# The mixer's output projection: its first two blocks as one pair, with three units of seven products, and the chunk ring's spare tiles kept on the raw side until the last block

## The chip, the cores and the metric

The kernel runs on one core of a Trainium2 chip. The metric is the device time of the whole program in microseconds (us). Engines are named as in the profile: PE is the matrix engine (PEld its weight loads), DVE the vector engine, ACT the scalar engine, POOL the GpSimd engine, SP the engine that only issues transfers.

## The reference

One layer of a decoder trunk on 256 tokens of width 2048, in float32. Cut to what the change touches:

```python
merged = sigmoid(gA) * (o_a @ w_o_mla) + sigmoid(gB) * (o_b @ w_o_swa)   # 256 x 2048
y = merged @ w_out                                                       # 2048 x 2048 weights
x = x + rms_norm(y, norm_mix_post)
x = x + rms_norm(conv_ffn(rms_norm(x, norm_ffn_pre), w_up, conv_w, conv_b, w_down), norm_ffn_post)
```

Everything before it (input projection, two attentions, gates) and after it (a gated feed-forward block of width 5632) stays as it is.

## The kernel before

**Products in three passes.** Each float32 operand is held as a high part and a low part. `mm3` (lines 173 to 177) makes one product from three matmuls: high x high (L175), high x low (L176), low x high (L177). A weight chunk of 128 x 1024 goes through four hands: a DMA issued by SP brings it into a tile `raw` (L131); ACT copies it to `whi` (L143); DVE subtracts to get `wlo` (L144); PE uses both.

**The ring.** `raw`, `whi` and `wlo` come in turn from one pool: three `raw` tiles (RAW), four of each of the others (RING), and two more tiles of a tag `flex`. While `flex[0]` is "raw" these two serve as a fourth and fifth `raw` tile; when it is "w", they serve as one more `whi` and one more `wlo` turn. In the kernel before, `flex` is "raw" up to the output projection and is set to "w" ahead of its first block.

**gemm** multiplies all 256 tokens (two tiles of 128, `acc[0]` and `acc[1]`) with 512 columns: 8 chunks of two 128-row slices, 96 matmuls of 512 columns, and a `tick()` after each chunk. `at(t, f)` hands a piece of work over to a later tick, so transposes and evacuations are written between the chunks.

**pair_gemm** exists already, for the gates and for the down projection. It computes 1024 columns at once, with four accumulators `c` (tokens x column halves) and four more, `q`, in the other PSUM banks. Its `order` string lists units of 256 weight rows: "p" is a plain unit (2 rows of chunks x 4 products of three matmuls, 24 matmuls), "s" a unit of seven products (21 matmuls, a Strassen-like scheme). A unit of seven needs sums of the activations made ahead (`token_sums`), loads its two chunks `even` and `odd` by POOL's queue (L227, L228), and has DVE make four sums of weight halves (L232 to L235). At the end of the last unit of seven, `first_sums` and `more_sums` add the `q` accumulators up (L255 to L261).

**The stages around the change.** In the merge stage each of four blocks `j` multiplies the attention output with `w_o_mla` (gemm), while `merge_loads` fetches the gate `lta` and the other branch `lyb` by POOL's queue (L943, L944); DVE combines them with the accumulator (L955, L956); `m_cols` transposes the result on PE (L935, tile `mT`) and splits it into `mth`, `mtl` (tiles `ahl`). Then come four blocks of 512 columns of `w_out`, each a gemm; `y_evac` squares the accumulator on ACT and multiplies it on DVE with the gain `gpost` into `yg` (L972, L973). `gpost` (four transfers) and the residual `x2` (eight) are loaded by SP's queue during the first half of the merge stage (`late_loads`). In the last block all of token tile 0 is done first and token tile 1 after it, so its weights are held; its first three chunks use tiles of their own (pool `px`). `resid` then makes the residual, its transposes and the norm. The engine queues are in order; the tile framework lists each engine's rows by its own priorities, so a row can stand earlier than its place in the text.

Of the kernel before, what the change touches and what calls it, by code (L numbers as in the profile page):

```python
# [23 lines left out]
KT = D // P  # L24
# [17 lines left out]
def trunk_layer(ctx, tc, x, x_cols_in, conv_cols_in, g_mix_post, g_ffn_post, w_in, w_q, w_kv,  # L42
                sinks, rel, wo_a, wo_b, w_out, w_up, w_down, rope_tab, strip_sel, out):
    nc = tc.nc
    vec, act, pe, pool = nc.vector, nc.scalar, nc.tensor, nc.gpsimd

    def open_pool(name, bufs=1, **kw):
        es = ExitStack()
        return es, es.enter_context(tc.tile_pool(name=name, bufs=bufs, **kw))
# [3 lines left out]
    pss = ctx.enter_context(tc.tile_pool(name="pss", bufs=2, space=PS))  # L53
# [5 lines left out]
    def sb(pl, shape, name, dt=F32, tag=None, bufs=None):  # L59
        return pl.tile(shape, dt, name=name, tag=tag or name, **({"bufs": bufs} if bufs else {}))  # L60
# [43 lines left out]
    flex = ["raw"]  # L104
    turn = dict(raw=0, w=0)
# [49 lines left out]
    now = [0]  # L155

    def at(t, *fs):
        steps[max(t, now[0])].extend(fs)
# [6 lines left out]
    def drain():  # L165
        while steps:
            tick()
# [11 lines left out]
    def gemm(xh, xl, w, k0, nk, c0, n, split=None, extra=None, ps=None):  # L179

        kc = 1024 // n if n in (256, 512) else 2
        acc = new_acc("g", ps)
        todo = []
        cuts = list(range(0, nk, kc)) + [nk]
        for ci, (k, ke) in enumerate(zip(cuts[:-1], cuts[1:])):
            kk = ke - k
            src = w[(k0 + k) * P:(k0 + k + kk) * P, c0:c0 + n].rearrange("(a p) n -> p a n", p=P)
            hi, lo = wchunk(src, [kk, n], *(extra or {}).get(ci, ()))
            for j in range(kk):
                kt = k + j  # L190
# [473 lines left out]
    acc, _ = gemm(XH, XL, w_in, 0, KT, 0, 512)  # L664
# [4 lines left out]
    acc, _ = gemm(XH, XL, w_in, 0, KT, C_KV, KVR + ROPE)  # L669
# [78 lines left out]
    AH, AL = pair_view(ath), pair_view(atl)  # L748
# [138 lines left out]
    b = now[0] + 26  # L887
# [11 lines left out]
    for j in range(4):  # L899
        acc, _ = gemm(XH, XL, w_in, 0, KT, C_GA + 512 * j, 512)  # L900
# [16 lines left out]
    gpost = sb(p6, [P, D], "gpost", tag="gp")  # L917

    def late_loads(i):

        if i < 4:
            nc.sync.dma_start(gpost[:, i * 512:(i + 1) * 512], g_mix_post[i * 512:(i + 1) * 512].partition_broadcast(P))
        else:
            t, j = divmod(i - 4, 4)
            nc.sync.dma_start(x2[t][j], x[t * P:(t + 1) * P, j * 512:(j + 1) * 512])

    esx, px = open_pool("px", bufs=EXTRA)
    es4, p4 = open_pool("p4")

    def m_cols(p, ld):  # L930
        pt = pst.tile([P, 512], F32, name=f"mT{p}", tag="t")
        for i in range(2):
            for t in range(NT):
                c = (2 * (p % 2) + i) * P
                pe.transpose(pt[:, i * 256 + t * P:i * 256 + (t + 1) * P], ld[t][0][:, c:c + P], ident)  # L935
        split_to(mth[p][:, :], mtl[p][:, :], pt, 0.5)
# [8 lines left out]
            ld.append((a, b))  # L945
        return ld

    for i in range(12):
        at(now[0] + 10 + 2 * i, lambda i=i: late_loads(i))
    for j in range(4):  # L950
        ld = merge_loads(j)
        acc, _ = gemm(AH, AL, wo_a, 0, KT, 512 * j, 512)
        for t in range(NT):
            a, b = ld[t]
            vec.scalar_tensor_tensor(a, a, 1.0, acc[t], op0=ALU.add, op1=ALU.mult)  # L955
            vec.tensor_tensor(a, a, b, op=ALU.add)  # L956
# [4 lines left out]
    yg_all = [[sb(p6, [P, 1024], f"yg_{t}_{j}", tag="f" + "ab"[t], bufs=2) for j in range(2)] for t in range(NT)]  # L961
    yg = [[yg_all[t][j // 2][:, (j % 2) * 512:(j % 2 + 1) * 512] for j in range(4)] for t in range(NT)]
    blocks = [(0, 512), (512, 512), (1024, 512), (1536, 256), (1792, 256)]
    NB = len(blocks)
    W_BLOCKS = [(512 * j, 512) for j in range(4)]
    ssy = [sb(p3, [P, 4], f"ssy{t}") for t in range(NT)]
    jk = lambda name: sb(p6, [P, 512], name, tag="jk", bufs=1)

    def y_evac(acc, b, t):
        c0, n = W_BLOCKS[b]  # L970
        j, o = c0 // 512, c0 % 512
        act.activation(jk(f"yj{b}_{t}")[:, :n], acc[t][:, :n], AF.Square, accum_out=ssy[t][:, b:b + 1])  # L972
        vec.tensor_tensor(yg[t][j][:, o:o + n], acc[t][:, :n], gpost[:, c0:c0 + n], op=ALU.mult)  # L973

    x2hl = [slot("b", p) for p in range(8)]
    HH, HL = pair_view(highs(x2hl)), pair_view(lows(x2hl))
# [31 lines left out]
        vec.tensor_scalar(r2, r, 0.5, None, op0=ALU.mult)  # L1008
        rf[t] = (r, r2)

    flex[0] = "w"
    turn.update(raw=0, w=0)
    for b in range(4):
        c0, n = W_BLOCKS[b]
        last = b == 3
        acc, todo = gemm(MH_, ML_, w_out, 0, KT, c0, n, split=0 if last else None, extra={i: (px,) for i in range(EXTRA)} if last else None)
        if b == 0:
            drain()
            es4.close()
            es8, p8 = open_pool("p8")  # L1020
        if last:
# [311 lines left out]
EXTRA = 3  # L1333
# [69 lines left out]
```

## Time and profile before

| | |
|---|---|
| median of 3 runs | 1468.9 us (1468.19 to 1469.03) |
| the profiled execution: its own time | 1470.05 us |
| its span, first to last instruction | 1468.3 us |
| granted PE clock in it | 0.998 |
| PE busy in the span | 1456.9 us (99%), 7576 matmuls |
| DVE busy | 1067.2 us (73%) |
| ACT busy | 830.5 us (57%) |
| the 32 loads of `w_out`, first and last issue | 623.9 us and 709.2 us |

The profile gives the engines' busy time by group of instructions, what ended an engine's idle time, and the chain of work that ended last. A matmul's record is longer than its share of PE's time, because matmuls overlap, so PE's pace is read from the starts of matmuls that follow each other, not from the length of one.

### The profile page before, as it was taken

What the parts mean: (1) busy time and instruction counts of PE and PEld (TensorE: products, weight loads), DVE (VectorE), ACT (ScalarE), POOL (GpSimd) and SP (SyncE); (2) the same over time, 40 slices, a digit from 0 to 9 for tenths busy, and PEclk for the clock granted to TensorE, in tenths of its full rate; (3) what the DMA queues carried; (4) which work ended last, traced back from release to release, by engine and by line L of the source; (5) the groups of instructions that cost most, each with busy time, mean ns of one, the idle gap of its engine ahead of it and who ended that gap; (6) DMA issues with size and microseconds to landing.
All of it is one profiled execution on the core that took longest, in us unless ns stands there. A gap on an engine that the chain in (4) does not pass through costs nothing.

```text
span 1468.3 us, 20938 instructions
## 1 busy us (share of the span) xinstructions
PE 1456.9 (99%) x7576; PEld 1244.8 (85%) x7576; DVE 1067.2 (73%) x1881; ACT 830.5 (57%) x1372; POOL 64.9 (4%) x113
## 2 busy tenths in 40 slices
PE   9999999999999999999999999999999999999997
PEld 7888888888888888888888888888888888888886
DVE  7688896745667665555699976778776687677775
ACT  7588874543555554444566655555454565555453
POOL 0011110000000000000000000000000000000000
PEclk9999999999999999999999999999999999999999
DMA  8755376466655559756766666665656666667573
GB/s 297 211 164 167 108 259 192 162 212 200 191 156 160 164 163 334 226 184 212 225 205 185 188 193 193 187 187 187 218 174 213 198 187 189 187 197 233 163 237 129
DMA packets 149909, 287.60 MB, mean 196 GB/s; under 512 B 18428, under 2 KB 29597, under 8 KB 149677
## 3 DMA queue, kind: packets, MB, share of 16 engines
q1 hardware_dynamic: 141312, 256.80, 56.5%
q0 software_dynamic: 8400, 29.41, 6.4%
q8 instruction: 59, 0.97, 0.3%
q14 instruction: 46, 0.37, 0.1%
q10 hardware_dynamic: 92, 0.05, 0.0%
HBM read 277.79 MB, written 8.44 MB: 195 GB/s over the span
## 4 chain that ended last, share of the span: by engine, by line
PE 97%; DVE 2%; ACT 1%; issue 0%; DMA 0%; DVEq 0%; ACTq 0%
PE accg L175 13%; PE accg L177 13%; PE accg L176 13%; PE ub L1147 10%; PE ua L1147 10%; PE ua L1151 5%; PE ub L1151 5%; PE cd L177 2%; PE cd L175 2%; PE cd L176 2%; PE cdb L175 1%; PE cdb L177 1%; PE cdb L176 1%; PE mpo L875 1%; PE cg L176 1%; PE cg L177 1%
## 5 line engine op out<-in xcount | busy, mean ns | idle before, releaser
L144 DVE TENSOR_TENSOR wlo<-raw,whi 128x1024 fp32r<-128x1024 f32 (+2 forms) x476 | 576.3, 1214 | 282.5 <-ACT whi L143 275.2
L143 ACT CAST whi<-raw 128x1024 fp32r<-128x1024 f32 (+2 forms) x476 | 494.7, 1043 | 427.5 <-PE accg L177 172.3
L175 PE MATMUL accg<-whi,ahl 128*128 128x512 f32 (+1 forms) x480 | 187.9, 392 | 0.0
L177 PE MATMUL accg<-whi,ahl 128*128 128x512 f32 (+1 forms) x480 | 185.6, 387 | 0.0
L176 PE MATMUL accg<-wlo,ahl 128*128 128x512 f32 (+1 forms) x480 | 184.8, 385 | 0.0
L1147 PE MATMUL ua<-ahl,whi 128*128 128x512 f32 x640 | 154.6, 391 | 0.0
L1147 PE MATMUL ub<-ahl,whi 128*128 128x512 f32 x640 | 154.6, 391 | 0.0
L175 PE MATMUL accg<-whi,bhl 128*128 128x512 f32 x378 | 148.2, 392 | 0.0
L177 PE MATMUL accg<-whi,bhl 128*128 128x512 f32 x378 | 147.4, 390 | 0.0
L176 PE MATMUL accg<-wlo,bhl 128*128 128x512 f32 x378 | 147.3, 390 | 0.0
L1147 PEld LDWEIGHTS ub<-ahl,whi 128*128 128x128 f32 x640 | 117.5, 188 | 22.9 <-ACT cc L1045 0.2
L1147 PEld LDWEIGHTS ua<-ahl,whi 128*128 128x128 f32 x640 | 117.6, 188 | 22.7
L177 PEld LDWEIGHTS accg<-whi,ahl 128*128 128x128 f32 x480 | 90.1, 188 | 18.0
L176 PEld LDWEIGHTS accg<-wlo,ahl 128*128 128x128 f32 x480 | 90.3, 188 | 15.6
L175 PEld LDWEIGHTS accg<-whi,ahl 128*128 128x128 f32 x480 | 90.3, 188 | 15.5
L1151 PEld LDWEIGHTS ub<-ahl,wlo 128*128 128x128 f32 x640 | 82.2, 191 | 3.2
L1151 PEld LDWEIGHTS ua<-ahl,wlo 128*128 128x128 f32 x640 | 82.2, 191 | 3.1
L1151 PE MATMUL ua<-ahl,wlo 128*128 128x256 f32 x640 | 83.7, 283 | 0.0
L177 PEld LDWEIGHTS accg<-whi,bhl 128*128 128x128 f32 x378 | 71.0, 188 | 14.8
L176 PEld LDWEIGHTS accg<-wlo,bhl 128*128 128x128 f32 x378 | 71.0, 188 | 14.5
L1151 PE MATMUL ub<-ahl,wlo 128*128 128x256 f32 x640 | 83.2, 283 | 0.0
L175 PEld LDWEIGHTS accg<-whi,bhl 128*128 128x128 f32 x378 | 71.0, 188 | 14.3
(545 smaller groups left out, 2218.9 us busy)
## 6 DMA issues: line engine op xcount, KB each, us to landing
raw<-in_ffn_w_up_dram SPq DMA_DIRECT2D x176, 512.0 KB, 4.5
raw<-in_w_in_dram SPq DMA_DIRECT2D x105, 512.0 KB, 4.5
raw<-in_ffn_w_down_dram SPq DMA_DIRECT2D x68, 512.0 KB, 4.5
raw<-in_w_o_swa_dram SPq DMA_DIRECT2D x32, 512.0 KB, 4.4
raw<-in_w_o_mla_dram SPq DMA_DIRECT2D x32, 512.0 KB, 4.5
raw<-in_w_out_dram SPq DMA_DIRECT2D x32, 512.0 KB, 4.1
bias<-strip POOLq DMA_DIRECT2D x16, 256.0 KB, 4.4
raw<-in_mla_w_q_up_dram SPq DMA_DIRECT2D x32, 128.0 KB, 2.8
```

The lines of the kernel that those rows point to most:

```text
L143: act.copy(hi[:, a:b], raw[:, a:b])
L144: vec.tensor_tensor(lo[:, a:b], raw[:, a:b], hi[:, a:b].bitcast(F32), op=ALU.subtract)
L175: pe.matmul(o, ah, bh, start=start, stop=False)
L176: pe.matmul(o, ah, bl, start=False, stop=False)
L177: pe.matmul(o, al, bh, start=False, stop=stop)
L875: pe.matmul(o, w(t), p_[:, c], start=n == 0, stop=n == 5)
L1147: pe.matmul(acc[i], hi[:, c], hn[p][:, j * 512:(j + 1) * 512], start=p + j == 0, stop=stop)
L1151: pe.matmul(acc[i][:, 0:256], lo[:, c], hn[p][:, j * 512:j * 512 + 256], start=False, stop=False)
```

## The change

Three things are done. First, the first two blocks of the output projection (columns 0 to 1023) become one `pair_gemm` in the order `ppspspsp`: five plain units and three of seven products, the latter on the first six slices of the activations. Its raw chunks for the units of seven come by POOL's queue into tiles of `px` (first and third unit) and into the tile of `gpost` (second unit). The sums of the activations (`m_sums`, three times) are handed over to ticks of block 2 of the merge stage's `for` loop, though the rows of the first two stand earlier in DVE's queue; they go into tiles of `px`, with the first `yg` tile as scratch. A new `pair_evac` adds `c` and the sums, squares, and multiplies with `gpost`.

Second, because the second unit's chunks stand in its tile, `gpost` is loaded later, by POOL's queue instead of SP's, once that unit is through; the loads of `x2` keep their ticks. The last merge block's accumulator moves to the banks of the tag "s", and the third block of the output projection too.

Third, `flex` is switched to "w" ahead of the last block instead of the first. The pool p8, which the feed-forward block's first chunks use, is opened behind the pair.

```diff
     def late_loads(i):
         if i < 4:
-            nc.sync.dma_start(gpost[:, i * 512:(i + 1) * 512], g_mix_post[i * 512:(i + 1) * 512].partition_broadcast(P))
+            if i == 0:
+                gpost.append(sb(p6, [P, D], "gpost", tag="gp"))
+            pool.dma_start(gpost[0][:, i * 512:(i + 1) * 512], g_mix_post[i * 512:(i + 1) * 512].partition_broadcast(P))
...
+    def m_sums(u):
+        st = sb(px, [P, 1024], f"ms{u}", F32R, tag="w" + ("hi", "lo")[u % 2])
+        ms[u] = token_sums(mt[u].bitcast(F32), yg[0][0], yg[0][1], st[:, 0:512], st[:, 512:1024])
+
-    for i in range(12):
+    for i in range(4, 12):
         at(now[0] + 10 + 2 * i, lambda i=i: late_loads(i))
     for j in range(4):
         ld = merge_loads(j)
-        acc, _ = gemm(AH, AL, wo_a, 0, KT, 512 * j, 512)
+        if j == 2:
+            for u in range(W_ORDER.count("s")):
+                at(now[0] + 2 + 4 * u, lambda u=u: m_sums(u))
+        acc, _ = gemm(AH, AL, wo_a, 0, KT, 512 * j, 512, ps=(pss, "s") if j == 3 else None)
...
-            at(now[0] + (3 if j == 3 else 1) + p, lambda p=2 * j + p, ld=ld: m_cols(p, ld))
+            at(now[0] + (2 if j == 3 else 1) + p, lambda p=2 * j + p, ld=ld: m_cols(p, ld))
...
-    flex[0] = "w"
-    turn.update(raw=0, w=0)
-    for b in range(4):
+    def w_place():
+        w_done[0] += 1
+        i = w_done[0]
+        if i % 2:
+            return [sb(px, [P, 1024], f"mr{i}{n}", tag="w" + n) for n in ("hi", "lo")]
+        both = sb(p6, [P, D], f"mr{i}", tag="gp")
+        at(now[0] + 2, *(lambda k=k: late_loads(k) for k in range(4)))
+        return both[:, 0:1024], both[:, 1024:2048]
+
+    def w_pair():
+        d = [yg[t][j] for t in range(NT) for j in range(2)]
+        c = pair_gemm("w", w_out, 0, 0, W_ORDER, lambda k, t: (MH_(k)[:, t * P:(t + 1) * P], ML_(k)[:, t * P:(t + 1) * P]),
+                      lambda u: ms[u], 0, d, w_place, lambda: [yg_all[t][1] for t in range(NT)])
+
+        def pair_evac(i):
+            t, j = divmod(i, 2)
+            vec.tensor_tensor(d[i], d[i], c[i], op=ALU.add)
+            act.activation(jk(f"yj{j}_{t}"), d[i], AF.Square, accum_out=ssy[t][:, j:j + 1])
+            vec.tensor_tensor(d[i], d[i], gpost[0][:, j * 512:(j + 1) * 512], op=ALU.mult)
+
+        for i in range(4):
+            at(now[0] + i, lambda i=i: pair_evac(i))
+
+    w_pair()
+    es4.close()
+    es8, p8 = open_pool("p8")
+    for b in range(2, 4):
...
-        acc, todo = gemm(MH_, ML_, w_out, 0, KT, c0, n, split=0 if last else None, extra={i: (px,) for i in range(EXTRA)} if last else None)
-        if b == 0:
+        if last:
+            flex[0] = "w"
+            turn.update(raw=0, w=0)
+        acc, todo = gemm(MH_, ML_, w_out, 0, KT, c0, n, split=0 if last else None, extra={i: (px,) for i in range(EXTRA)} if last else None,
+                         ps=None if last else (pss, "s"))
...
+W_ORDER = "ppspspsp"
```

What this makes of the engines' rows is shown at three places. The names `mr1`, `mr2` (printed as `mr_6759`) and `mr3` are the raw chunks of the three units of seven, `hi` and `lo` there standing for the even and the odd row.

POOL's queue in the merge stage, before: behind the two stores of the last gate come only the gates and branches of blocks 1 to 3.

```order
L904 DMA ta_d<-ta_0_5832 128x512
L904 DMA ta_d<-ta_1_5835 128x512
L944 DMA lyb_0_6022<-yb_d 128x512
L944 DMA lyb_1_6026<-yb_d 128x512
L943 DMA lta_1_6025<-ta_d 128x512
L943 DMA lta_0_6196<-ta_d 128x512
L944 DMA lyb_0_6197<-yb_d 128x512
L944 DMA lyb_1_6201<-yb_d 128x512
L943 DMA lta_1_6200<-ta_d 128x512
L943 DMA lta_0_6372<-ta_d 128x512
L944 DMA lyb_0_6373<-yb_d 128x512
L944 DMA lyb_1_6377<-yb_d 128x512
```

The same stretch of POOL's queue after; one load of the second unit's chunk stands just ahead of these rows.

```order
L228 DMA mr_6759<-in_w_out_dram 128x1024
L946 DMA lyb_0_6025<-yb_d 128x512
L946 DMA lyb_1_6029<-yb_d 128x512
L945 DMA lta_1_6028<-ta_d 128x512
L945 DMA lta_0_6196<-ta_d 128x512
L228 DMA mr1lo<-in_w_out_dram 128x1024
L228 DMA mr3lo<-in_w_out_dram 128x1024
L946 DMA lyb_0_6197<-yb_d 128x512
L946 DMA lyb_1_6201<-yb_d 128x512
L945 DMA lta_1_6200<-ta_d 128x512
L945 DMA lta_0_6387<-ta_d 128x512
L227 DMA mr1hi<-in_w_out_dram 128x1024
```

Five of the six raw chunks for the units of seven have moved up into the merge stage, between the gates and branches; the sixth (`mr3hi`) and the four `gpost` loads follow behind the last `lta`.

DVE's queue at the end of merge block 2, before: conversions alone, and then the combination with the gate.

```order
L144 TENSOR_TENSOR wlo_6353<-raw_6350,whi_6352 128x1024
L144 TENSOR_TENSOR wlo_6385<-raw_6382,whi_6384 128x1024
L144 TENSOR_TENSOR wlo_6404<-raw_6401,whi_6403 128x1024
L144 TENSOR_TENSOR wlo_6429<-raw_6426,whi_6428 128x1024
L955 SCALAR_TENSOR_TENSOR lta_0_6196<-lta_0_6196,accg_0_6204 128x512
```

The same place after, from the last sums of the activations on.

```order
L284 TENSOR_TENSOR yg_0_5862<-yg_0_5862 128x128
L318 TENSOR_TENSOR ms_6460<-yg_0_5862,ms_6460 128x512
L144 TENSOR_TENSOR wlo_6368<-raw_6365,whi_6367 128x1024
L232 TENSOR_TENSOR yg_1_5863<-mr1hi 128x512
L144 TENSOR_TENSOR wlo_6400<-raw_6397,whi_6399 128x1024
L233 TENSOR_TENSOR yg_1_5863<-mr1lo,mr1hi 128x512
L234 TENSOR_TENSOR yg_1_5865<-mr1lo,yg_1_5863 128x512
L235 TENSOR_TENSOR yg_1_5865<-mr1lo,yg_1_5865 128x512
L144 TENSOR_TENSOR wlo_6419<-raw_6416,whi_6418 128x1024
L144 TENSOR_TENSOR wlo_6444<-raw_6441,whi_6443 128x1024
```

The first unit's weight sums (L232 to L235) have moved in between the conversions, so the conversions behind L232 are queued behind the landing of `mr1hi`.

DVE's queue around the end of the first two blocks, before, from the evacuation of block 1 on.

```order
L973 TENSOR_TENSOR yg_0_6548<-accg_0_6735,gpost 128x512
L973 TENSOR_TENSOR yg_0_6550<-accg_1_6736,gpost 128x512
L144 TENSOR_TENSOR wlo_6964<-raw_6961,whi_6963 128x1024
L144 TENSOR_TENSOR wlo_6982<-raw_6979,whi_6981 128x1024
L144 TENSOR_TENSOR wlo_7000<-raw_6997,whi_6999 128x1024
```

The same place after, from the first conversion of the pair's last plain unit on (`qw` and `cw` are the accumulators `q` and `c` of the pair).

```order
L144 TENSOR_TENSOR wlo_6892<-raw_6889,whi_6891 128x1024
L144 TENSOR_TENSOR wlo_6913<-raw_6910,whi_6912 128x1024
L256 TENSOR_TENSOR yg_0_5862<-yg_0_5862,qw_6689 128x512
L144 TENSOR_TENSOR wlo_6939<-raw_6936,whi_6938 128x1024
L257 TENSOR_TENSOR yg_0_5864<-yg_0_5862,qw_6688 128x512
L144 TENSOR_TENSOR wlo_6961<-raw_6958,whi_6960 128x1024
L260 TENSOR_TENSOR yg_0_5864<-yg_0_5864,qw_6687 128x512
L261 TENSOR_TENSOR yg_0_5862<-yg_0_5862,qw_6687 128x512
L1040 TENSOR_TENSOR yg_0_5862<-yg_0_5862,cw_6583 128x512
L1040 TENSOR_TENSOR yg_0_5862<-yg_0_5862,cw_6584 128x512
L144 TENSOR_TENSOR wlo_6983<-raw_6980,whi_6982 128x1024
```

Two evacuations per block have become four sums over `q`, and then an addition and a multiplication for each of four parts; L260 and L261 free the bank that block 2's second accumulator uses.

More of the change, by code (lines that the diff above doesn't have):

```diff
@@ L916, in trunk_layer @@
     es6, p6 = open_pool("p6")
-    gpost = sb(p6, [P, D], "gpost", tag="gp")
+    gpost = []
     def late_loads(i):
         if i < 4:
-            nc.sync.dma_start(gpost[:, i * 512:(i + 1) * 512], g_mix_post[i * 512:(i + 1) * 512].partition_broadcast(P))
+            if i == 0:
+                gpost.append(sb(p6, [P, D], "gpost", tag="gp"))
+            pool.dma_start(gpost[0][:, i * 512:(i + 1) * 512], g_mix_post[i * 512:(i + 1) * 512].partition_broadcast(P))
         else:
@@ L946, in merge_loads @@
         return ld
-    for i in range(12):
+    yg_all = [[sb(p6, [P, 1024], f"yg_{t}_{j}", tag="f" + "ab"[t], bufs=2) for j in range(2)] for t in range(NT)]
+    yg = [[yg_all[t][j // 2][:, (j % 2) * 512:(j % 2 + 1) * 512] for j in range(4)] for t in range(NT)]
+    ms = {}
+    def m_sums(u):
+        st = sb(px, [P, 1024], f"ms{u}", F32R, tag="w" + ("hi", "lo")[u % 2])
+        ms[u] = token_sums(mt[u].bitcast(F32), yg[0][0], yg[0][1], st[:, 0:512], st[:, 512:1024])
+    for i in range(4, 12):
         at(now[0] + 10 + 2 * i, lambda i=i: late_loads(i))
@@ L957, in trunk_layer @@
         for p in range(2):
-            at(now[0] + (3 if j == 3 else 1) + p, lambda p=2 * j + p, ld=ld: m_cols(p, ld))
-    yg_all = [[sb(p6, [P, 1024], f"yg_{t}_{j}", tag="f" + "ab"[t], bufs=2) for j in range(2)] for t in range(NT)]
-    yg = [[yg_all[t][j // 2][:, (j % 2) * 512:(j % 2 + 1) * 512] for j in range(4)] for t in range(NT)]
+            at(now[0] + (2 if j == 3 else 1) + p, lambda p=2 * j + p, ld=ld: m_cols(p, ld))
     blocks = [(0, 512), (512, 512), (1024, 512), (1536, 256), (1792, 256)]
@@ L972, in y_evac @@
         act.activation(jk(f"yj{b}_{t}")[:, :n], acc[t][:, :n], AF.Square, accum_out=ssy[t][:, b:b + 1])
-        vec.tensor_tensor(yg[t][j][:, o:o + n], acc[t][:, :n], gpost[:, c0:c0 + n], op=ALU.mult)
+        vec.tensor_tensor(yg[t][j][:, o:o + n], acc[t][:, :n], gpost[0][:, c0:c0 + n], op=ALU.mult)
     x2hl = [slot("b", p) for p in range(8)]
@@ L1009, in x2_norm @@
         rf[t] = (r, r2)
-    flex[0] = "w"
-    turn.update(raw=0, w=0)
-    for b in range(4):
+    w_done = [0]
+    def w_place():
[21 more added lines that the diff above has]
+    for b in range(2, 4):
         c0, n = W_BLOCKS[b]
         last = b == 3
-        acc, todo = gemm(MH_, ML_, w_out, 0, KT, c0, n, split=0 if last else None, extra={i: (px,) for i in range(EXTRA)} if last else None)
-        if b == 0:
+        if last:
[3 more added lines that the diff above has]
+                         ps=None if last else (pss, "s"))
+        if last:
             drain()
-            es4.close()
-            es8, p8 = open_pool("p8")
-        if last:
             y_evac(acc, b, 0)
```

## The prediction, as put on record before the change was run

> **What bounds the kernel now.** I read the engines' shares first, then the chain of waits, then the engines' waits and the stretches around the change.
>
> ```profile
> span 1468.3 us, 20938 instructions
> PE 1456.9 (99%) x7576; PEld 1244.8 (85%) x7576; DVE 1067.2 (73%) x1881; ACT 830.5 (57%) x1372; POOL 64.9 (4%) x113
> PEclk9999999999999999999999999999999999999999
> PE 97%; DVE 2%; ACT 1%; issue 0%; DMA 0%; DVEq 0%; ACTq 0%
> ```
>
> PE is busy 99% of the span, at a full granted clock, and 97% of the chain that ended last is PE's. So time is saved only by fewer or shorter matmuls, and lost only where PE is made to stand. The waits from the second merge block to the end of the output projection (550 to 727 us) agree.
>
> ```profile
> ACT whi L143 <- PE accg L177: 67.3, 42, 2.2
> ACT whi L143 <- DMA raw<-in_w_out_dram: 18.4, 12, 3.3
> PEld x2T L990 <- issue: 0.5, 1, 0.5
> ```
>
> The columns are total, count and longest. ACT waits for PE (42 times), in the output projection also for loads (12 times), but of PE's own waits only 0.5 us at the residual's transposes shows. Everything else hides behind PE. What a matmul costs is read from PE's timeline in block 1 of the output projection, first and last of 197 rows:
>
> ```profile
> 659.69 0.40 PE L177 MATMUL accg<-whi,ahl 128*128 128x512 f32 x1
> ...
> 704.12 0.39 PE L175 MATMUL accg<-whi,ahl 128*128 128x512 f32 x1
> ```
>
> 196 intervals in 44.43 us are 0.2267 us from start to start.
>
> **The change, part by part: PE.** Two blocks are 2 x 96 = 192 matmuls of 512 columns. The pair has five plain units of 24 and three of 21, 183 in all. Nine fewer, at 0.2267 us, are **-2.04 us**. The Trainium skill ("TensorE: Matmul & The Clock Gate", section "Wait — 56ns, not 53.3ns?") gives 215.7 ns for this shape on a warm array; by it the saving would be 9 x 0.2157 = 1.94 us. The trace differs from it (0.2267), and the measurement decides.
>
> **DVE in the pair.** The gates' pair (216 to 285 us) has the same three units of seven and shows what these cost. By groups, by rows of the timeline, and by waits:
>
> ```profile
> L144 DVE TENSOR_TENSOR wlo<-gr,whi 128x512 fp32r<-128x512 f32 x3 | 2.1, 687 | 0.4 <-ACT whi L143 0.4
> L235 DVE TENSOR_TENSOR gtb<-gr,gtb 128x512 f32<-128x512 f32 x3 | 2.1, 685 | 0.0
> ...
> 252.01 4.62 DVE L144 TENSOR_TENSOR wlo<-raw,whi 128x1024 fp32r<-128x1024 f32 x4
> 621.48 1.29 DVE L956 TENSOR_TENSOR lta<-lta,lyb 128x512 f32<-128x512 f32 x2
> ...
> DVE gta L232 <- DMA gr<-in_w_in_dram: 1.8, 1, 1.8
> PEld cg L176 <- DVE wlo L144: 0.3, 1, 0.3
> ```
>
> Back to back a conversion of 1024 columns takes 4.62 / 4 = 1.16 us, an operation on 512 columns 1.29 / 2 = 0.65 (0.69 alone). A unit of seven asks three of the former and five of the latter, 6.7 us, while PE works 21 x 0.2267 = 4.8 us on it; a plain unit asks 2.3 of PE's 5.4. Seven and plain together are 9.0 of 10.2 us: DVE is late in a seven and catches up in the plain unit behind it. In the order ppspspsp each seven is followed by one plain unit, and two stand ahead. The whole pair asks 3 x 6.7 + 5 x 2.3 = 31.6 us of 41.5. In the gates this pattern cost PE one wait of 0.3 us.
>
> The tightest place is the handover to block 2: its second accumulator takes a bank of q, free only after L261. DVE does there, from the last plain unit's first conversion on, three more conversions and four sums of 512 columns: 3 x 1.16 + 4 x 0.65 = 6.1 us. PE reaches block 2's second accumulator 24 + 3 matmuls after it could start that unit, 27 x 0.2267 = 6.1 us. That leaves almost nothing beside what DVE has in hand from the unit before (1.2 us of 10.2). I bound the stall here by 0 and by 1.8 us (the load wait of L232 falling into this place), and take **+0.3 us**, the wait that the nearest row, the gates' pair, shows. Zero would need a reserve that the rows don't give.
>
> The rest of DVE's new work (three sets of token sums in merge block 2, the weight sums of the first unit, four sums and four additions at the evacuation) lies where DVE has room:
>
> ```profile
> 550.00:590.00 40.00, 40.00 (x182) 33.10 (x181) 20.66 (x20) 17.12 (x19) 4.23 (x8) 1.00 0.93 333
> 644.26:720.70 76.44, 76.44 (x343) 63.27 (x342) 42.84 (x41) 35.22 (x43) 0.00 (x0) 1.00 0.66 213
> ```
>
> The columns are us, then the busy time of PE, PEld, DVE, ACT and POOL, PE's clock, the DMA share and GB/s. DVE is busy 20.7 of 40 us in the merge stage and 42.8 of 76.4 in blocks 0 to 3, PE all of it. In the pair its load rises to about 32 of 41.5, still under PE. Cost nothing; if the cover were gone, each operation would cost its 0.65 us once.
>
> **Loads.** The bytes are the same; their place is not. Four `gpost` transfers (1.05 MB) leave SP's queue and the first half of the merge stage; five chunks of `w_out` (2.6 MB) enter the merge stage on POOL's queue, of which the second unit's two and `mr1lo`, `mr3lo` (2.1 MB) fall in its first three blocks. The crowded stretch is seen here by ten microseconds (same columns), with the landing times of the ring's chunks (550 to 600 us) and of the gates' POOL loads:
>
> ```profile
> 570.00:580.00 10.00, 10.00 (x46) 8.29 (x45) 6.87 (x8) 4.09 (x4) 1.09 (x2) 1.00 1.05 384
> 580.00:590.00 10.00, 10.00 (x50) 8.25 (x49) 5.22 (x6) 4.26 (x6) 1.06 (x2) 1.00 0.93 322
> ...
> DMA to landing us min/median/max: 3.7/5.7/7.3
> ...
> L227 POOL DMA_DIRECT2D gr<-in_w_in_dram x3: 528/542/564, 200.7 to 244.5; - x3
> DMA to landing us min/median/max: 4.0/5.4/7.7
> ```
>
> The 40 us moved 333 x 40 = 13.3 MB. Plus 2.1 minus 1.05 MB they are 14.4 MB, at the highest rate shown (384 GB/s) 37.4 us: tight, 2.6 us spare. A chunk of the ring is needed five tiles after its refill, 5 x 12 x 0.2267 = 13.6 us, against landings up to 7.3 us: a margin of 6 us. I take 0. The bounds are 0 and what rival 1 gives. The Trainium skill ("SBUF — State Buffer", section "A bandwidth-pool intuition that's wrong (but worth ruling out)") lists about 358 GB/s between HBM and a core; by it, as an estimate, 14.4 MB take 40.1 us, the stretch would be full and the first rival's way open. The trace disagrees with it as a limit: 384 GB/s stand in the row above.
>
> The one load on which other work queues is `mr1hi`: POOL issues it behind two `lta`, and DVE, in order, stands at L232 until it lands.
>
> ```profile
> 607.28 1.06 POOL L943 DMA_DIRECT2D lta<-ta_d  x2 [6.41 <-PE mT L935]
> 610.98 1.22 DVE L144 TENSOR_TENSOR wlo<-raw,whi 128x1024 fp32r<-128x1024 f32 x1 [1.38 <-ACT whi L143]
> 613.70 1.23 DVE L144 TENSOR_TENSOR wlo<-raw,whi 128x1024 fp32r<-128x1024 f32 x1 [1.50 <-ACT whi L143]
> 620.28 1.28 DVE L955 SCALAR_TENSOR_TENSOR lta<-lta,accg 128x512 f32<-128x512 f32 x2
> ```
>
> Issued at 608.4, with 4.0 to 7.7 us to landing, it is there at 612.4 to 616.1. DVE comes to L232 at about 612.5, behind the conversion of 610.98, so it waits 0 to 3.6 us. The conversion queued behind it (before, ended at 614.9) belongs to the last chunks of this block, whose end is the row at 620.28: 5.3 us of reserve. Cost 0; ACT, which waits for PE there, and the `raw` tiles follow with the same reserve.
>
> **Block 3.** The switch of `flex` moves from block 0 to block 3, which therefore starts with more raw chunks loaded but fewer converted.
>
> ```profile
> 711.19 1.05 ACT L143 CAST whi<-raw 128x1024 fp32r<-128x1024 f32 x1 [3.29 <-DMA raw<-in_w_out_dram]
> 715.35 1.21 DVE L144 TENSOR_TENSOR wlo<-raw,whi 128x1024 fp32r<-128x1024 f32 x1
> 720.70 0.60 ACT L972 ACTIVATE yj<-accg 128x512 f32<-128x512 f32 x1 [2.31 <-PE accg L177]
> ```
>
> Token tile 0 ends at 720.70; its last chunk is 6 matmuls, 1.36 us, and so begins at 719.3; its conversion ended at 716.6. The reserve is 2.7 us. One turn fewer ahead takes 1.4 of it, two take all. The two additional raw tiles give back: the load wait of 3.3 us in the first row came with three. I take 0 and bound it by 0 and by 2.0 us (a late load as in the gates, 1.8, rounded up).
>
> `gpost` comes behind the second unit on an otherwise idle POOL queue, and is first used at the pair's end, two units (10 us) and more later; with the landings above (at most 7.7) it is hidden.
>
> **Sum.** -2.04 + 0.3 = -1.74 us. The profiled execution took 1470.05 us, 1.75 around its span; it becomes 1468.3. It stands 1.15 above the median of the runs, 1468.9, which becomes **1467.2 us**. The most that the rows allow is 2.04 plus the 0.5 at the transposes, 2.5 us, or 1466.4.
>
> **The rivals.** *1, the other side: POOL's loads come late.* If the crowded merge stage delays `mr1hi`, DVE stands at L232 and every conversion behind it stands too. With twice the longest landing shown, 15.4 us, it lands at 623.8; DVE is held 11.3 us from 612.5, PE 11.3 - 5.3 = 6.0 us: 1468.9 - 2.04 + 6.0 = 1472.9. PE stands from a landing of about 9 us on, and the change is slower by 0.2% from about 14 us on (4.9 us of stall). For it: the share of 1.05 at 570 to 580, and 1 MB more in that stretch. Against it: `mr1hi` itself goes out at 608, behind the crowded stretch, and the gates' POOL loads landed within 7.7 us. A chance of 0.14.
>
> *2, DVE too slow in the pair.* If each of the three sevens and the handover lets PE stand by 0.3 to 0.5 us, or one load wait of 1.8 us falls at the handover, 1.5 to 2 us are lost and the time is 1468.4 to 1468.9. For it: 9.0 of 10.2 us. Against: 0.3 us in the gates. 0.10.
>
> *3, block 3 starved.* The full 2.0 us there: 1467.2 + 2.0 = 1469.2. For it: the reserve of 2.7 and ACT's load waits. Against: five raw tiles instead of three. 0.08.
>
> *4, more gain than the rows show*, over 2.9 us: something now waits that no record shows. 0.06.
>
> **How the numbers follow.** The sum has the remaining 0.62, with a range of its own from 1466.4 to 1467.9 (a stall of 1.0). A measurement of this kernel can tell about 0.2% from no change, 2.9 us, so the sum's gain lies within. Faster by more is rival 4, 0.06; slower by more is rival 1, 0.14; within are the sum, 2 and 3, 0.80. A range from 1466.2 to 1470.5 leaves out rivals 4 and 1, 0.20, and holds the upper end of 3 with half a stall of rival 2 on top.
>
> **What would show it.** Right: nine PE records fewer; PE's starts at 0.2267 us throughout the pair; at most a wait or two of PE for `wlo` or a q sum, below 0.5 us each; L232's wait for `mr1hi` under 5 us; no PE wait before token tile 0's end in block 3; span about 1466.6. Wrong: a PE wait for DVE at block 2's second accumulator over 1 us (2), PE standing in merge block 2 or 3 with DVE waiting for `mr` (1), or PE waiting for `whi` or `wlo` in block 3 (3).

## The result, and the profile after

| | before | after |
|---|---|---|
| median of 22 runs each | 1468.9 us | 1466.63 us |
| lowest to highest | 1467.86 to 1470.05 | 1465.11 to 1468.17 |
| ratio, 95% interval | | 0.9986 (0.998 to 0.9991) |
| profiled execution: own time, span | 1470.05, 1468.3 | 1466.82, 1464.7 |

The change gains 2.3 us, 0.14%; forecast was 1467.2. The page of the changed kernel begins:

```profile
span 1464.7 us, 20974 instructions
PE 1454.3 (99%) x7567; PEld 1242.8 (85%) x7567; DVE 1088.9 (74%) x1925; ACT 837.7 (57%) x1382; POOL 70.2 (5%) x123
PEclk9999999999999999999999999999999999999999
```

Nine PE records fewer (7567 for 7576), 2.6 us less of PE, 21.7 us more of DVE, and PE still 99% of the span. The two profiled spans differ by 3.6 us, more than the medians do, so the difference has to be placed. PE's timeline of the kernel before has the output projection's first matmul and the residual's first transpose:

```profile
643.31 0.39 PE L175 MATMUL accg<-whi,ahl 128*128 128x512 f32 x1
...
726.82 0.63 PE L990 MATMUL x2T<-ident,x 128*128 128x128 f32 x4
```

and that of the changed kernel the same two, with the first matmul behind the pair between them:

```profile
642.22 0.39 PE L175 MATMUL cw<-whi,ahl 128*128 128x512 f32 x1
...
684.67 0.39 PE L175 MATMUL accg<-whi,ahl 128*128 128x512 f32 x1
...
723.64 0.55 PE L1001 MATMUL x2T<-ident,x 128*128 128x128 f32 x3
```

The stage took 83.51 us and now takes 81.42: 2.09 us less, 2.04 of them the nine matmuls. Of the remaining 1.5 us of the spans' difference, 1.09 had arisen before the stage began and 0.4 lies behind it. The 1.09 is there before the first changed row of POOL's queue runs: POOL's last store of a gate (`ta_d`, L904) goes out at 554.5 us before and at 553.4 after. And flex_alone below, which has the kernel before's rows up to this stage, begins it at 642.01, not at 643.31. So the 1.09 belongs to the two executions; the 0.4 was not placed further. This is most of why the span came out below the 1466.6 that was forecast.

PE's, ACT's and DVE's waits that bear on the prediction, in the changed kernel from 600 to 727 us (total, count, longest):

```profile
ACT whi L143 <- PE accg L177: 28.0, 20, 1.7
ACT whi L143 <- PE cw L177: 17.9, 14, 2.1
ACT whi L143 <- DMA raw<-in_w_out_dram: 7.4, 6, 1.7
DVE yg L232 <- DMA mr1hi<-in_w_out_dram: 2.0, 1, 2.0
PEld x2T L1001 <- DVE x L998: 0.7, 2, 0.5
```

PE has no wait in the pair, nor in blocks 2 and 3; its only ones are again at the residual's transposes. ACT's waits for loads of `w_out` fell from 12 to 6.

### The profile page after: what moved, and what is told of

The parts are those of the page before. It is cut to its first block, busy times and chain, and to the rows that moved or that the text cites. A ratio compares the mean times of both kernels' runs of the same rounds, so it can differ in the third digit from the quotient of the medians.

```text
span 1464.7 us, 20974 instructions
## 1 busy us (share of the span) xinstructions
PE 1454.3 (99%) x7567; PEld 1242.8 (85%) x7567; DVE 1088.9 (74%) x1925; ACT 837.7 (57%) x1382; POOL 70.2 (5%) x123
## 4 chain that ended last, share of the span: by engine, by line
PE 94%; DVE 2%; issue 2%; ACT 1%; DMA 1%; POOL 0%; DVEq 0%; ACTq 0%; POOLq 0%
PE accg L175 12%; PE accg L177 12%; PE accg L176 12%; PE ua L1185 10%; PE ub L1185 10%; PE ua L1189 5%; PE ub L1189 5%; PE cd L177 2%; PE cd L175 2%; PE cd L176 2%; PE mpo L875 1%; PE cg L175 1%; PE cw L177 1%; PE cg L177 1%; PE cw L176 1%
## 5 line engine op out<-in xcount | busy, mean ns | idle before, releaser
L144 DVE TENSOR_TENSOR wlo<-raw,whi 128x1024 fp32r<-128x1024 f32 (+2 forms) x470 | 568.4, 1214 | 248.2 <-ACT whi L143 241.2
L143 ACT CAST whi<-raw 128x1024 fp32r<-128x1024 f32 (+2 forms) x470 | 487.9, 1043 | 405.0 <-PE accg L177 156.9
L175 PE MATMUL accg<-whi,ahl 128*128 128x512 f32 (+1 forms) x416 | 162.8, 391 | 0.0
L177 PE MATMUL accg<-whi,ahl 128*128 128x512 f32 (+1 forms) x416 | 160.6, 386 | 0.0
L176 PE MATMUL accg<-wlo,ahl 128*128 128x512 f32 (+1 forms) x416 | 159.8, 384 | 0.0
L177 PEld LDWEIGHTS accg<-whi,ahl 128*128 128x128 f32 x416 | 78.1, 188 | 15.4
L176 PEld LDWEIGHTS accg<-wlo,ahl 128*128 128x128 f32 x416 | 78.2, 188 | 13.1
L175 PEld LDWEIGHTS accg<-whi,ahl 128*128 128x128 f32 x416 | 78.2, 188 | 13.0
L175 PEld LDWEIGHTS accg<-whi,bhl 128*128 128x128 f32 x378 | 71.0, 188 | 14.4
```

Of the source, the lines that this page charges most:

```text
L143: act.copy(hi[:, a:b], raw[:, a:b])
L144: vec.tensor_tensor(lo[:, a:b], raw[:, a:b], hi[:, a:b].bitcast(F32), op=ALU.subtract)
L175: pe.matmul(o, ah, bh, start=start, stop=False)
L176: pe.matmul(o, ah, bl, start=False, stop=False)
L177: pe.matmul(o, al, bh, start=False, stop=stop)
```

## The experiments

Twelve kernels ran. The times are medians; the kernel before was run beside them on the same chip. Five theories stand against each other: A, the nine matmuls are the gain and the rest hides; B, the gain comes from the arrangement, the five raw tiles above all; C, the units of seven cost PE something that the arrangement gives back; D, DVE has far more room than the prediction gave it; E, the last transposes of the merge stage wait for a PSUM bank (the place of an accumulator) that they share with `q`, comes up on the way.

| run | time, us | before beside it | ratio, 95% interval |
|---|---|---|---|
| plain8 | 1468.3 | 1468.4 | 0.9999 (0.999 to 1.0008) |
| two_sevens | 1467.19 | 1468.4 | 0.9992 (0.9983 to 1.0001) |
| flex_alone | 1468.79 | 1468.4 | 1.0003 (0.9994 to 1.0012) |
| flex_early | 1468.16 | 1468.4 | 1.0 (0.9991 to 1.0009) |
| sevens_together | 1468.09 | 1468.55 | 0.9997 (0.9989 to 1.0006) |
| dve_held4 | 1466.68 | 1468.55 | 0.9987 (0.9978 to 0.9996) |
| dve_held9 | 1475.33 | 1468.55 | 1.0043 (1.0031 to 1.0056) |
| four_sevens_b | 1467.37 | 1468.55 | 0.9994 (0.9985 to 1.0003) |
| after_again | 1466.47 | 1468.45 | 0.9986 (0.9977 to 0.9995) |
| flex_mid | 1469.82 | 1468.45 | 1.0008 (0.9999 to 1.0017) |
| four_sevens_mt0 | 1465.54 | 1468.45 | 0.9982 (0.9973 to 0.9991) |
| four_sevens_d | 1465.93 | 1468.45 | 0.9982 (0.9973 to 0.9991) |

An interval is some 1.3 us to either side, so steps of 0.7 us are read from the traces, by the length of the pair's stretch on PE, or of the whole stage (from the first matmul of the output projection to the residual's first transpose, 81.42 us in the changed kernel). The changed kernel ran again beside flex_mid, four_sevens_mt0 and four_sevens_d only; the others are compared with it through the kernel before and through the traces.

### Is it the matmuls? plain8, two_sevens and after_again

plain8 keeps the pair and drops its units of seven (the evacuation then reads `c` alone, and `gpost` is loaded at a tick of the pair); two_sevens keeps two; after_again is the changed kernel.

```diff
-W_ORDER = "ppspspsp"
+W_ORDER = "pppppppp"    # plain8
+W_ORDER = "ppppspsp"    # two_sevens
```

> The first two blocks stay one pair with all that goes with it (banks, place of the switch of flex, gpost by POOL's queue), but in eight plain units: 192 matmuls, no sums. Theory A (the gain is the nine matmuls, and all else hides): 2.0 us slower than the changed kernel, within 0.5 us of the kernel before, 1468.9 us, and no wait of PE in the pair. Theory B (the gain comes from the arrangement, the five raw chunks above all): within 0.7 us of the changed kernel, 1466.6 us. Theory C (the units of seven cost PE something which the arrangement gives back): in between or below the changed kernel.

> The changed kernel with two units of seven in place of three (order ppppspsp): 186 matmuls in the pair, three more than in the changed kernel. Theory A: 3 x 0.2267 = 0.68 us slower than the changed kernel, 1.36 us faster than before, about 1467.4 us; seven columns of PE's records show 7570 matmuls. Theory B: as the changed kernel, 1466.6 us. Theory C: faster than the changed kernel.

> The changed kernel itself, as the yardstick on the chip of the three runs beside it: 2.0 to 2.3 us faster than before, and in the trace 2.04 us fewer between the merge stage's start and the residual.

PE's timeline, the pair's first matmul and the first one behind it, in plain8:

```profile
641.44 0.39 PE L175 MATMUL cw<-whi,ahl 128*128 128x512 f32 x1
...
685.93 0.39 PE L175 MATMUL accg<-whi,ahl 128*128 128x512 f32 x1
```

in two_sevens:

```profile
641.53 0.39 PE L175 MATMUL cw<-whi,ahl 128*128 128x512 f32 x1
...
684.66 0.39 PE L175 MATMUL accg<-whi,ahl 128*128 128x512 f32 x1
```

The stretch takes 44.49 us with no unit of seven, 43.13 with two, 42.45 with three (642.22 to 684.67 above). That is 0.68 us for each, three matmuls at 0.2267 us, to the hundredth, so no unit of seven costs PE anything beside. plain8's time is that of the kernel before. Theory C falls, and theory B falls as the source of the gain. after_again repeats the result with a ratio of 0.9986.

### Are the five raw tiles needed? flex_alone, flex_early, flex_mid

flex_alone is the kernel before with the switch moved to the last block and nothing else. flex_early and flex_mid are the changed kernel with the switch elsewhere:

```diff
-        if last:                 # in the loop over blocks 2 and 3
-            flex[0] = "w"
-            turn.update(raw=0, w=0)
...
+    flex[0] = "w"                # flex_early: ahead of w_pair()
+    turn.update(raw=0, w=0)
...
+        if b == 2:               # flex_mid: one block earlier
+            flex[0] = "w"
+            turn.update(raw=0, w=0)
```

> The kernel before with one edit: the two spare tiles stay raw tiles until the last block of the output projection. Theory A: within 0.5 us of the kernel before; ACT's twelve waits for loads of w_out (18.4 us) become fewer in blocks 0 to 2, and PE does not notice. Theory B: at least 1 us faster than before.

> The changed kernel with the switch of flex back ahead of the first of these blocks, so that the pair has three raw tiles and one converted turn more. Theory A: within 0.5 us of the changed kernel, 1466.6 us; ACT's waits for loads of w_out become more, PE has none in the pair. Theory B: 1.5 to 2 us slower, back at 1468.5 us.

> The changed kernel with the switch of flex ahead of its third block: five raw tiles in the pair, three in the third and the last block. With the switch ahead of the pair PE waited 1.2 us for the last conversion of the last block. If the loads fall behind in the pair and at its handover, five raw tiles there suffice: no wait, 1466.6 us. If the three raw tiles limit the loads in the third block (a tile each 2.4 us, one third of load, copy and subtraction), PE waits 0.5 to 1.2 us in the last block: 1467.1 to 1467.8 us.

In flex_alone ACT's waits for loads of `w_out` fell from 18.4 us to

```profile
ACT whi L143 <- DMA raw<-in_w_out_dram: 2.1, 4, 0.8
```

and the time did not move (1.0003), as theory A said. flex_early was not as A said: by the medians it loses most of the gain, and in the trace its stage takes 82.74 us (641.66 to 724.40) instead of 81.42. Its waits (PE's from 590 to 760 us, ACT's from 550 to 727), and the row of PE's timeline at which the long one ends, with the row of ACT's timeline that makes the copy this chunk needs:

```profile
PEld accg L176 <- DVE wlo L144: 1.1, 1, 1.1
PEld x2T L1001 <- DVE x L998: 0.9, 2, 0.7
PEld accg L175 <- ACT whi L143: 0.2, 1, 0.2
ACT whi L143 <- DMA raw<-in_w_out_dram: 13.9, 11, 2.2
...
716.62 0.50 PE L176 MATMUL accg<-wlo,ahl 128*128 128x512 f32 x1 [0.76 <-DVE wlo L144]
...
714.26 1.05 ACT L143 CAST whi<-raw 128x1024 fp32r<-128x1024 f32 x1 [1.42 <-DMA raw<-in_w_out_dram]
```

PE stands at the last chunk of token tile 0 in block 3: it waits for DVE's subtraction, that for ACT's copy, and the copy had waited for its load. Nothing is lost in the pair itself (42.46 us). The loads show why. Of the `w_out` chunks behind the pair's own, first and last issue in flex_early and in the changed kernel:

```profile
L131 SPq DMA_DIRECT2D raw<-in_w_out_dram x16: 367/368/378, 667.6 to 709.5; - x16
```

```profile
L131 SPq DMA_DIRECT2D raw<-in_w_out_dram x16: 367/368/379, 659.6 to 708.1; - x16
```

With the spare tiles on the raw side the sixteen loads start 8 us earlier, and the last one 1.4 us earlier; flex_early stands for 1.2 us. flex_mid is worse than either:

```profile
PEld accg L176 <- DVE wlo L144: 3.7, 4, 1.1
PEld x2T L1001 <- DVE x L998: 1.9, 3, 0.9
...
ACT whi L143 <- DMA raw<-in_w_out_dram: 13.3, 8, 3.2
```

Four waits of PE in block 3, and a time 3.3 us above after_again. Both readings that were written for it expected at most 1.2 us. That three raw tiles hold up the loads behind the pair is shown by both runs: ACT waits 13.9 and 13.3 us for them, against 7.4 in the changed kernel. Such waits need not cost time: the kernel before has 18.4 us of them, and PE doesn't stand. Why a switch between the pair and block 2 costs more than one ahead of the pair was not tried apart and stays open.

So the five raw tiles save nothing by themselves and are a condition of the gain: the pair takes 2.04 us from PE's time and none from that of the loads, and without the two spare tiles the last block pays 1.2 us of it back. How far the shorter pair is the cause of this is taken up below, at block 3.

### What covers DVE? sevens_together

```diff
-W_ORDER = "ppspspsp"
+W_ORDER = "ppppsssp"
```

> The changed kernel in the order ppppsssp: the same 183 matmuls, but the three units of seven without a plain unit between them, and one plain unit behind them. Theory A with DVE's need as the prediction has it (6.7 us in a seven against PE's 4.8, so 5.8 us behind after three, less what DVE has in hand): PE waits for DVE 1 to 4 us in the pair, the time is 1467.6 to 1470.6 us. Theory D (DVE has far more room than those rows say): no wait, 1466.6 us.

The waits from 640 to 690 us, and PE's row at which the longest ends:

```profile
ACT whi L143 <- DVE yg L233: 2.4, 1, 2.4
PEld qw L175 <- ACT whi L143: 1.6, 2, 1.0
ACT whi L143 <- DVE yg L235: 1.1, 2, 0.8
...
677.69 0.50 PE L175 MATMUL qw<-whi,ms 128*128 128x512 f32 x1 [0.61 <-ACT whi L143]
```

In the third of the three, ACT waits for DVE's weight sums (L233, L235) and PE for ACT. The pair's stretch takes 43.78 us (641.75 to 685.53) instead of 42.45, so 1.3 us are lost there, and 1.7 in the whole stage (641.75 to 724.87). Both lie inside the 1 to 4 us that the prediction's 6.7 against 4.8 us gave, at its low end. Theory D falls: with three units of seven in a row PE waits, and in the changed kernel the plain units between them are what hides DVE. Whether two may stand side by side is seen in the next section.

### A fourth unit of seven: four_sevens_b, four_sevens_mt0, four_sevens_d

```diff
-W_ORDER = "ppspspsp"
+W_ORDER = "psspspsp"                    # four_sevens_b and _mt0
+W_ORDER = "ppsspssp"                    # four_sevens_d
...
-        at(now[0] + 2, *(lambda k=k: late_loads(k) for k in range(4)))
+        if i == 4:
+            at(now[0] + 2, *(lambda k=k: late_loads(k) for k in range(4)))
...
-            vec.tensor_tensor(d[i], d[i], gpost[0][:, j * 512:(j + 1) * 512], op=ALU.mult)
+            at(now[0] + 4, lambda: vec.tensor_tensor(d[i], d[i], gpost[0][:, j * 512:(j + 1) * 512], op=ALU.mult))
...
-            at(now[0] + (2 if j == 3 else 1) + p, lambda p=2 * j + p, ld=ld: m_cols(p, ld))
+            at(now[0] + (0 if j == 3 else 1) + p, lambda p=2 * j + p, ld=ld: m_cols(p, ld))   # four_sevens_mt0 alone
```

> A fourth unit of seven (order psspspsp, 180 matmuls, gpost loaded behind the fourth, the gain's multiplications four ticks later). By matmuls alone 0.68 us faster than the changed kernel, 1465.9 us. Theory A with DVE's need: two sevens side by side and 4 x 6.7 + 4 x 2.3 = 36 us of 40.8, so PE waits 1 to 2 us and the time is 1467 to 1468 us. Theory D: 1465.9 us.

> The kernel with four units of seven (psspspsp) and one edit: the last merge block's transposes are handed over two ticks earlier, ahead of the first unit of seven. There PE had waited 1.7 us at the last of these transposes, whose bank is one of q's and came free only with the sum on L256. Theory E (that bank was the whole loss): the waits go, 180 matmuls, 0.68 us faster than the changed kernel, 1465.9 us, faster than both. Theory A with DVE's need (36 us of 40.8, two sevens side by side): 1 to 2 us of waits stay, 1467 to 1468 us.

> Four units of seven in the order ppsspssp, the transposes where the changed kernel has them: two plain units ahead, so the transposes keep ahead of q, but two pairs of sevens without a plain unit between them. Theory E: no wait at the transposes; 1465.9 us if DVE keeps up, each pair of sevens puts DVE 3.8 us behind and its copies and subtractions in hand (some 3.5 us) just cover it; PE waits 0 to 1 us, 1465.9 to 1466.9 us. Theory A with DVE's need: 1 to 3 us of waits, 1467 to 1469 us.

four_sevens_b came out at 1467.37, as theory A had it, but not for A's reason. PE's timeline at the end of its pair:

```profile
678.16 0.51 PE L175 MATMUL accg<-whi,ahl 128*128 128x512 f32 x1 [0.17 <-ACT whi L143]
679.07 0.66 PE L937 MATMUL mT<-ident,lta 128*128 128x128 f32 x4 [0.41 <-DVE yg L256]
680.21 0.50 PE L176 MATMUL accg<-wlo,ahl 128*128 128x512 f32 x1 [0.47 <-DVE wlo L144]
```

These transposes (`mT`) belong to the merge stage and should be done 25 us earlier. Their bank is one of `q`'s, which the first unit of seven takes after one plain unit, before the last transposes were handed over; they then wait for the sum at L256. four_sevens_mt0 hands them over two ticks earlier and changes nothing else, and its stretch on PE is

```profile
641.39 0.39 PE L175 MATMUL cw<-whi,ahl 128*128 128x512 f32 x1
...
683.17 0.39 PE L175 MATMUL accg<-whi,ahl 128*128 128x512 f32 x1
```

41.78 us, 0.67 less than with three units of seven, with no wait in the pair: theory E holds. The whole stage takes 80.74 us here (641.39 to 722.13) and 82.79 in four_sevens_b (641.73 to 724.52), so the place of the transposes was worth 2.05 us. DVE keeps up, though two sevens stand side by side and it is busy 37.8 of the 41.78 us (36 of 40.8 were expected), so theory A was too strict there. four_sevens_d brings the pair to 41.89 us by its order (642.25 to 684.14), with 0.2 us of PE waits in it. In its profiled execution later waits give this back (0.2 us in block 3, 1.6 at the residual's transposes): its stage takes 81.47 us, as long as the changed kernel's. four_sevens_mt0 is the fastest of all kernels here: 1465.54 us beside 1466.47 of after_again and 1468.45 of before, with its interval clear of the kernel before; that it is ahead of the changed kernel is carried by the trace (0.67 us), since the two intervals overlap.

### What does a late chunk cost? dve_held4 and dve_held9

The prediction's first rival, on the slower side, had DVE held in merge block 2 by a late `mr1hi`. One added DVE operation on `mr1hi` takes the place of the lateness; it reads the tile four or nine times over and puts a sum that nothing uses into a column which is overwritten later.

```diff
+            if name == "w" and u == 0:
+                with tc.high_priority(400):
+                    vec.tensor_reduce(ssh[0][:, 0:1], even[:, None, :].to_broadcast([P, 4, 1024]), axis=AX.XY, op=ALU.add)
             vec.tensor_tensor(ta[:, lo_], even[:, hi_], even[:, lo_], op=ALU.subtract)
```

> The changed kernel with one added DVE operation ahead of the first weight sum of the first unit of seven: it reads mr1hi four times over (4096 columns, worked out from the conversions' 1.14 us per 1024 columns as some 4.5 us) and holds DVE's queue in merge block 2 as a later landing of mr1hi would. Theory A: a conversion behind it has some 3.4 us left beyond the 2.0 us wait seen, so PE waits 0 to 1 us: 1466.6 to 1467.6 us. Rival (the reserve of 5.3 us isn't there): 3 to 4.5 us slower than the changed kernel.

> The same with nine times over (9216 columns, some 10 us): a stand-in for mr1hi landing some 16 us after its issue, the first rival's case. Theory A: PE waits 6 to 8 us in merge block 3, the time is 1472.6 to 1474.6 us, slower than before by over 0.2%. Rival (the list order lets the conversions pass, or the reserve is larger): under 1469 us.

DVE's timeline in dve_held4:

```profile
613.61 4.42 DVE L234 TENSOR_REDUCE ssh<-mr1hi 128x1 f32<-128x4096 f32 x1 [2.77 <-DMA mr1hi<-in_w_out_dram]
617.94 3.48 DVE L144 TENSOR_TENSOR wlo<-raw,whi 128x1024 fp32r<-128x1024 f32 x3
```

The added row makes the lines behind it three higher, so L235, L971 and L940 here are L232, L968 and L937 of the changed kernel. DVE comes free at 618.0 us, and the time stays (1466.68). PE has one wait for it:

```profile
PEld accg L176 <- DVE wlo L144: 0.5, 1, 0.5
```

The executions are shifted against each other by up to 1.8 us here, so the hold is counted from the end of the conversion ahead of it, 610.8 us in this run: DVE is held 7.2 us. With the prediction's reserve of 5.3 us PE would stand 1.9 us. It stands 0.5, so the reserve is there and larger, some 6.7 us. In dve_held9 DVE's and PE's timelines read:

```profile
614.69 9.75 DVE L234 TENSOR_REDUCE ssh<-mr1hi 128x1 f32<-128x9216 f32 x1 [3.01 <-DMA mr1hi<-in_w_out_dram]
624.36 1.27 DVE L971 SCALAR_TENSOR_TENSOR lta<-lta,accg 128x512 f32<-128x512 f32 x2
```

```profile
626.38 1.84 PE L940 MATMUL mT<-ident,lta 128*128 128x128 f32 x7 [6.18 <-DVE lta L972]
...
630.32 0.63 PE L176 MATMUL accg<-wlo,bhl 128*128 128x512 f32 x1
630.75 0.60 PE L177 MATMUL accg<-whi,bhl 128*128 128x512 f32 x1
```

DVE comes free at 624.4, as if `mr1hi` had landed there. The conversion ahead ended at 611.7, so DVE is held 12.8 us, and a reserve of 5.3 gives 7.5 us of standing. PE stood 6.2 us, which makes the reserve 6.6 us, and then the matmuls started 0.43 us apart instead of 0.23 until 631.2. The pair begins at 651.14 us instead of 642.22: together some 9 us are lost in the trace. The time is 1475.33, above the 1472.6 to 1474.6 expected. The list of DVE's rows also changed (the combinations with the gate, L971 and L972, went ahead of conversions), so the run isn't a pure delay, and PE stood ahead of the transposes (`mT`) that need a combination, not at a conversion. But a long hold of DVE at this place does stop PE at the end of merge block 2, from a somewhat longer hold on than the rival said. What kept the rival away is that `mr1hi` came in time.

## Why the prediction was right, point by point

**The nine matmuls: right to the hundredth.** -2.04 us forecast; plain8 against the changed kernel, 44.49 - 42.45, gives 2.04. The 1.94 by the Trainium skill ("TensorE: Matmul & The Clock Gate", section "Wait — 56ns, not 53.3ns?") was the worse figure.

**The stall at the handover: 0.3 us forecast, none found.** DVE's timeline in the changed kernel has the sum that frees the bank,

```profile
683.80 0.68 DVE L261 TENSOR_TENSOR yg<-yg,qw 128x512 f32<-128x512 f32 x1
```

and PE's the first matmul that needs it:

```profile
685.35 0.39 PE L175 MATMUL accg<-whi,ahl 128*128 128x512 f32 x1
```

The bank was free at 684.48, 0.87 us ahead. The mis-sized term is what DVE has in hand when the last plain unit begins; I had it at nearly nothing, and the gates' 0.3 us did not carry over. Without it the sum is 1466.86, within 0.25 us of the median.

**DVE in the pair: right, a little low.** About 32 us of 41.5 were forecast. A table of windows of the changed kernel (columns as in the prediction) has 34.1 of 42.45 in the last row, which is the pair's stretch with the merge stage's last transposes in it:

```profile
570.00:580.00 10.00, 10.00 (x48) 8.31 (x47) 7.08 (x8) 3.50 (x4) 1.08 (x2) 1.00 1.05 391
550.00:590.00 40.00, 40.00 (x182) 33.11 (x181) 24.50 (x32) 18.47 (x21) 5.36 (x10) 1.00 0.94 337
642.22:684.67 42.45, 42.45 (x192) 35.14 (x191) 34.10 (x40) 22.87 (x25) 2.66 (x5) 1.00 0.50 158
```

That the plain units are its cover was shown by taking them away (1.3 us lost in the pair). The need of 6.7 us for a seven was a little on the safe side: read from start to start in the changed kernel, a conversion takes 1.13 us (659.49 to 660.62) and a sum 0.60 (653.41 to 654.01), 6.4 us for a seven. The fourth unit shows that with what DVE has in hand even two sevens side by side are covered.

**The loads: right in result, wrong in the bytes.** The crowded 40 us (second row above) moved 337 x 40 = 13.5 MB, not 14.4: part of what the change adds there lands outside the stretch (`mr3lo`, issued at 585.0, took 7.9 us). 391 GB/s stand at 570 to 580, again above the 358 of the Trainium skill ("SBUF — State Buffer", section "A bandwidth-pool intuition that's wrong (but worth ruling out)"), so that figure was no limit over these 10 us. The landings became longer, though PE didn't notice. The ring's chunks from 550 to 600 us took

```profile
DMA to landing us min/median/max: 4.3/7.3/9.9
```

where the kernel before had 3.7/5.7/7.3, so the margin of 6 us that the prediction worked out shrank to 3.7. `mr1hi` was issued at

```profile
607.25 0.53 POOL L227 DMA_DIRECT2D mr1hi<-in_w_out_dram  x1
```

and DVE went on at 613.56, when it had landed, after a wait of 2.0 us: 0 to 3.6 were forecast, with 4.0 to 7.7 us for the landing.

**Block 3: nothing lost, as taken, but the step was read the wrong way round.** I treated the late switch of `flex` as a burden on block 3, bounded by 2 us, and the two more raw tiles as a relief on the side. flex_early shows the opposite: the late switch is what keeps PE from standing 1.2 us there. So the zero was right partly by luck: the step that was charged with the cost is the one that prevents it. The prediction looked at each part of the change against the kernel before, and missed that the shorter pair itself takes PE's time away from the loads. The reserve was forecast at 0 to 1.3 us. ACT's and DVE's timelines give it:

```profile
717.57 0.60 ACT L983 ACTIVATE yj<-accg 128x512 f32<-128x512 f32 x1 [1.62 <-PE accg L177]
```

```profile
713.90 1.23 DVE L144 TENSOR_TENSOR wlo<-raw,whi 128x1024 fp32r<-128x1024 f32 x1 [1.48 <-ACT whi L143]
```

The last conversion ends at 715.1, the last chunk of token tile 0 (1.36 us) begins at 716.2: 1.1 us. That the shorter pair takes from this reserve fits plain8, which has the pair and the late switch, but all 192 matmuls (and no sums for DVE). Its last conversion ahead of that chunk is in the row

```profile
712.18 2.35 DVE L144 TENSOR_TENSOR wlo<-raw,whi 128x1024 fp32r<-128x1024 f32 x2
```

and so ends at 714.5 at the latest, 2.9 us before the chunk begins (717.5). With nine matmuls fewer it is 1.1 us here and 1.6 in after_again. But the matmuls are not the whole account. With three raw tiles the kernel before had 2.7 us of reserve and flex_early has 1.2 us of standing, 3.9 us apart, of which the nine matmuls are 2.04. What the rest is was not tried apart.

**The rivals.** 1 did not happen. Held long enough, DVE does stop PE there, from a hold of some 6.6 us instead of 5.3 (dve_held4, dve_held9); its price was too low, since PE's clock falls after a long stand. 2 did not happen; taking the cover away brings it, and the 1.3 us then lost in the pair lie near its 1.5. 3 did not happen; its place and the late loads were right, but the late switch that it feared is what keeps it away. 4 did not happen: what the medians have beyond 2.04 us is 0.2 us, and no row carries it.

## What to carry to other kernels

In this kernel, where PE is 99% of the span, matmuls that fall away were worth their number times their pace, as long as each engine and each load that feeds PE gets its work done in the shorter time: look for what was just in time before (here the loads of the last block), and give it more room in the same change. A unit that loads another engine more than PE needs lighter ones near it (here two in a row were covered, three were not), and its place counts for PSUM banks too: a fourth such unit lost its gain to a transpose that shared a bank with it, and got it back when the transpose was written two ticks earlier.

## What the hardware showed that I had not expected

After PE had stood for 6.2 us in dve_held9, its granted clock was halved for a while. The windows of that run show the clock in the third column from the end:

```profile
610.00:619.00 9.00, 9.00 (x42) 7.44 (x41) 5.73 (x3) 3.58 (x4) 0.00 (x0) 1.00 0.54 198
626.38:631.18 4.80, 4.80 (x15) 3.70 (x15) 4.80 (x6) 0.60 (x1) 1.61 (x3) 0.50 0.57 167
632.00:642.00 10.00, 10.00 (x46) 8.19 (x45) 7.08 (x9) 4.70 (x5) 0.00 (x0) 1.00 0.89 320
```

0.50 for 4.8 us behind the stand, and 1.00 before and after; the matmuls' starts, 0.43 and 0.23 us apart, say the same. The stand of 6.2 us so cost about 9. Waits up to 1.1 us (flex_early, flex_mid) left the pace behind them at 0.23. The Trainium skill ("TensorE: Matmul & The Clock Gate", section "HAM oscillation — how this bites in real kernels") says that idle gaps of PE should stay under about 3.4 us; the run agrees that 6.2 us is beyond the limit, and none here has a stand between 1.3 (plain8, behind this stage) and 6.2 us that would place it.
